# An output product begun before the last gate, modulation columns placed behind the emitted blocks, and a norm whose small operations read PSUM

## The chip, the cores and the metric

The kernel runs on one core of one Trainium2 chip. The metric is the device time of one execution in microseconds (us). Engines are named as the profile names them: PE (TensorE, matmuls; PEld loads its weights), DVE (VectorE), ACT (ScalarE), POOL (GpSimd) and SP, which here only issues DMAs. SBUF is the on-chip memory, PSUM the banks into which PE writes and from which DVE and ACT read; POOL does not touch PSUM here.

## What is computed

A two-layer backbone on 512 tokens of width 1024. Layer 0 mixes tokens with a state-space branch (SSD) and eight heads of gated linear attention (GLA); layer 1 with a convolution module. A convolutional gated MLP follows each. Both sub-blocks end in a residual and a layer norm, and per-channel modulation columns are made from the conditioning vector:

```python
for l in range(DEPTH):                                   # DEPTH = 2
    m = (s_c @ ada_w[l] + ada_b[l]).reshape(-1, 6, 1, D_MODEL)
    h = modulate(x, m[:, 0], m[:, 1])
    if l % 2 == 0:
        y, yc = even_mixer(h, hc, mix_w_in[e], ..., mix_w_out[e], ctx_next)
    else:
        y = conformer_conv(h, *conf)
    x = layer_norm(ALPHA * x + m[:, 2] * y, post_ln_g[l, 0], post_ln_b[l, 0])
    x = layer_norm(ALPHA * x + m[:, 5] * conv_glu_ffn(modulate(x, m[:, 3], m[:, 4]), *ffn, rows, GRID_W),
                   post_ln_g[l, 1], post_ln_b[l, 1])

def merge(s, y, o):                                      # end of even_mixer
    ys = rms_norm(y * silu(z), ssd_nw, SSD_GROUPS)
    os_ = rms_norm(o, hg_nw, HG_HEADS) * silu(g)
    return concatenate([ys, os_], axis=-1) @ w_out
```

## The kernel before

Activations lie channel-major: a 1024-wide tensor is eight tiles of 128 channels by 512 tokens. Every fp32 product is made of three matmuls on operands split into a high and a low part: high weight times high activation, high times low, low times high (L214 to L216, `mm3w`, weights stationary; L233 to L235, `mm3a`, activations stationary). The weights come as one stream of 128x512 tiles in a fixed order: SP loads `wraw`, ACT casts the high part `whi` (L184), and the low part `wlo` (L188) is a subtraction on DVE, or on POOL once `lo_pool` is set.

A modulation column is made by `ada` (L266 to L274): a 512 KB DMA into one of two `ada` buffers and one DVE instruction (L273) of 128x1024 with an accumulator. `ada_some(n)` issues the next n columns of a list, to follow the instruction that `self.after` names. Before, each GLA head takes one at each of its seven levels, `merge` takes 16, and the FFN of layer 0 the rest.

A GLA head ends with levels (`lev` matmuls; L746 copies them under a mask into `p`; L748 to L754 update `kq` and `t`), then, for two directions, transposes of `kq` (`pk`, L764), a copy to `kt` (ACT L766), state updates (`pu`, L769) and outputs (`po`). `merge` then emits 16 blocks of the output product's activations (transposes `pt`, L818; `ohi` on ACT, L821; `olo` on DVE, L822), the last four after a gate whose second factor `sg` comes from the last projection (`psz`) and whose multiplications are L791. The output product runs 16 blocks deep over five columns into five PSUM banks (`psg`), then the residuals (L903) free them, and `project` makes the three other columns: one whole (`ps`), two by halves of 256 tokens (`psh`).

The norm is made by halves as well. `ln_add` accumulates the sum and the sum of squares (`a`, L924 and L925). `ln_sums` has PE sum over channels (`sm`, L938), then a chain of small DVE operations on 128x2 (mean, variance, and a reciprocal root by three Newton steps, `rsqrt`, L255 to L261). `ln_spread` has PE spread mean and root over the channels (`pb`, L954), and `normalise` applies them (L1019 and L1020; in the last norm L959 and L960), with the split for the next product (L1022 to L1027). `stats_later(n1, n2)` inserts sums and spreading behind so many of the `mm3w` calls of the product that runs meanwhile; `post` does it for the second half inside the next product.

The program is written in one order; a scheduler then sets the order of each engine's instructions by its own model, within what the buffers, the data and `issue_after` allow. Each engine runs its instructions in that order.

Of the kernel before, what the change touches and what calls it, by code (L numbers as in the profile page):

```python
# [17 lines left out]
P = 128  # L18
# [129 lines left out]
class Net:  # L148
# [104 lines left out]
    def rsqrt(self, y, v, tmp, itmp):  # L253
# [4 lines left out]
        for _ in range(3):  # L258
            ve.tensor_tensor(out=tmp, in0=y, in1=y, op=ALU.mult)
            ve.scalar_tensor_tensor(out=tmp, in0=tmp, scalar=-0.5, in1=v, op0=ALU.mult, op1=ALU.mult)  # L260
            ve.scalar_tensor_tensor(out=y, in0=tmp, scalar=1.5, in1=y, op0=ALU.add, op1=ALU.mult)  # L261
# [422 lines left out]
    def gla(self, h, v, act, actc, qs, o, so, gp, gd, mm, lv, mi):  # L684
# [53 lines left out]
        while m < P:  # L738
# [16 lines left out]
            if lev < self.ADA_HEAD:  # L755
                self.ada_some(1)
# [27 lines left out]
    ADA_HEAD, ADA_OUT, ADA_DOWN = 7, 16, 5  # L784
# [8 lines left out]
    def merge(self, mx, ox, y, o, so, acth):  # L793
# [9 lines left out]
        mm = ps_.enter_context(self.pool("mm", 5, PSUM))  # L803
# [10 lines left out]
        def emit(src, wname, half, off):  # L814
            for i in range(4):
# [6 lines left out]
                nc.vector.scalar_tensor_tensor(out=olo[:, n, :], in0=pt[:].rearrange("p c t -> p (c t)"), scalar=col,  # L822
# [7 lines left out]
        for c, ps in enumerate(proj(C_G, 1)):  # L830
            nc.scalar.activation(out=sg[:, c, :], in_=ps, func=AF.Silu)
        self.gate(o, sg, r, 4, 4)
# [6 lines left out]
        es = self.es  # L839
        self.x = es.enter_context(self.pool("x", side="right")).tile([P, KT, T], F32, name="x")  # L840
        self.work = es.enter_context(self.pool("work", 4, side="right"))
        self.mm = es.enter_context(self.pool("mm", 5, PSUM))
        self.lnps = es.enter_context(self.pool("lnps", 1, PSUM))
        for k in range(KT):
            nc.sync.dma_start(out=self.x[:, k, :], in_=self.A["xT"][k])
            nc.scalar.mul(self.x[:, k, :], self.x[:, k, :], ALPHA)
        self.lo_pool = True
        ln = self.ln_start()
        bk = [self.mm.tile([P, T], F32, tag="mm", name="psg") for _ in range(NW1)]
        self.ada_some(self.ADA_OUT)  # L850
        for k in range(16):
            for i in range(NW1):
                self.mm3w(bk[i], self.wblock(("wout", k * P, i * P)), (ohi[:, k, :], olo[:, k, :]), k == 0, k == 15)
# [9 lines left out]
    def project(self, ln, w, act, kt, layer, j, tail, then=None, first=0):  # L863
# [10 lines left out]
        for t0, t1 in HALVES:  # L874
# [8 lines left out]
            if t1 < T:  # L883
                self.stats_later(ln, t0, t1, 6, 8)
# [45 lines left out]
    def ln_sums(self, ln, t0, t1):  # L930
# [4 lines left out]
        sm = self.lnps.tile([P, 2 * n], F32, tag="sm", name="sm")  # L935
# [5 lines left out]
        nc.vector.tensor_scalar_mul(st, sm, 1.0 / D)  # L941
        mu = st[:, 0:n]
        nc.vector.tensor_tensor(out=tmp, in0=mu, in1=mu, op=ALU.mult)
        nc.vector.scalar_tensor_tensor(out=v, in0=st[:, n:], scalar=EPS, in1=tmp, op0=ALU.add, op1=ALU.subtract)
# [305 lines left out]
```

## Time and profile before

| quantity | value |
|---|---|
| runs of the kernel, median (lowest to highest) | 1761.66 us (1760.66 to 1762.17) |
| profiled execution, its own time | 1762.31 us |
| its span | 1760.5 us |
| mean granted PE clock | 0.99 |
| instructions in the trace | 26474 |
| modulation column DMAs | 104 of 512 KB, 3.6 us to landing |
| weight tile DMAs | 488 of 256 KB, 2.7 us to landing |

Busy shares are averages over stages. What bounds a stage is read from the waits of the engine that is busiest there, and from windows that show the granted clock beside the busy times. In a timeline row stand the start, the duration, engine, line, operation and tiles, and in brackets the idle time before it with the instruction that ended it.

### The profile page before, as it was taken

To read this page: it belongs to the slowest core of one execution; us is meant where nothing else is said; L and a number is where in the kernel's file an instruction comes from. 1 tells how busy PE (TensorE), PEld (TensorE's weight loads), DVE (VectorE), ACT (ScalarE), POOL (GpSimd) and SP (SyncE) were. 2 spreads that over 40 slices of the span, in tenths; PEclk is the share of its full clock that TensorE was granted. 3 is DMA by queue.
4 is the path that set the end of the run, shared out by engine and by line. 5 is a ranking of instruction groups with operands and counts; after the bars stand their busy time and mean duration, and the time that the engine had idled before them with its cause. 6 is when DMAs were issued, how large, how long until landed. Compare 5 with 4: busy or idle time off the path is not lost. (4 is left out here: it accounts for less than half of the span.)

```text
span 1760.5 us, 26474 instructions
## 1 busy us (share of the span) xinstructions
PE 1707.3 (97%) x9574; PEld 1465.3 (83%) x9574; DVE 1247.9 (71%) x2368; ACT 850.5 (48%) x1713; POOL 525.8 (30%) x436
## 2 busy tenths in 40 slices
PE   6999999999999999999999999999999999999996
PEld 5987768989899987887888888988898888888886
DVE  7778988969695996378777731488788777776125
ACT  4556775354444544364333422499534743333233
POOL 4400000000000003544444444533415444444451
PEclk9999999999999999999999999999999999999998
DMA  9621102434343448423333333322203233333331
GB/s 365 239 66 48 31 19 89 135 119 154 109 144 120 133 139 277 134 85 114 108 108 108 109 112 96 102 73 60 61 26 90 85 96 98 100 96 96 96 107 61
DMA packets 92194, 194.02 MB, mean 110 GB/s; under 512 B 10496, under 2 KB 13568, under 8 KB 92064
## 3 DMA queue, kind: packets, MB, share of 16 engines
q1 hardware_dynamic: 92016, 192.21, 35.0%
q8 instruction: 75, 1.23, 0.3%
q14 instruction: 55, 0.45, 0.1%
q0 software_dynamic: 48, 0.13, 0.0%
HBM read 190.21 MB, written 2.10 MB: 109 GB/s over the span
## 5 line engine op out<-in xcount | busy, mean ns | idle before, releaser
L188 POOL TENSOR_TENSOR wlo<-wraw,whi 128x512 fp32r<-128x512 f32 x388 | 510.0, 1318 | 1188.5 <-ACT whi L184 1171.6
L184 ACT CAST whi<-wraw 128x512 fp32r<-128x512 f32 x488 | 300.9, 619 | 509.2 <-PE ps L215 254.0
L214 PE MATMUL ps<-h1hi,whi 128*128 128x512 f32 x768 | 299.9, 391 | 2.0 <-DVE acc L1066 1.9
L216 PE MATMUL ps<-h1hi,wlo 128*128 128x512 f32 x768 | 299.6, 390 | 0.6 <-POOL wlo L188 0.6
L215 PE MATMUL ps<-h1lo,whi 128*128 128x512 f32 x768 | 299.6, 390 | 0.0
L1066 DVE SCALAR_TENSOR_TENSOR acc<-ps,pcol,acc 128x441 f32<-128x441 f32 (+2 forms) x320 | 222.4, 695 | 57.5 <-ACT acc L1058 47.9
L214 PEld LDWEIGHTS ps<-h1hi,whi 128*128 128x128 f32 x768 | 144.5, 188 | 32.2 <-ACT acc L1058 2.3
L216 PEld LDWEIGHTS ps<-h1hi,wlo 128*128 128x128 f32 x768 | 144.6, 188 | 31.2 <-POOL wlo L188 1.1
L215 PEld LDWEIGHTS ps<-h1lo,whi 128*128 128x128 f32 x768 | 144.7, 188 | 29.5
L273 DVE CUSTOM_DVE_ANT_0 junk<-ada,sc,pcol 128x1024 bf16<-128x1024 f32 x80 | 105.8, 1322 | 14.8 <-DMA ada<-adaw 14.6
L903 DVE SCALAR_TENSOR_TENSOR x<-ps,mod,x 128x512 f32<-128x512 f32 x14 | 10.5, 750 | 146.7 <-PE ps L216 146.7
L215 PE MATMUL ps<-glo,whi 128*128 128x512 f32 x264 | 102.7, 389 | 0.0
L214 PE MATMUL ps<-ghi,whi 128*128 128x512 f32 x264 | 102.7, 389 | 0.0
L216 PE MATMUL ps<-ghi,wlo 128*128 128x512 f32 x264 | 102.7, 389 | 0.0
L1158 DVE SCALAR_TENSOR_TENSOR cr<-u,pcol,cr 128x511 f32<-128x511 f32 (+20 forms) x156 | 97.7, 699 | 1.7 <-ACT cr L1141 1.5
L214 PE MATMUL ps<-hhi,whi 128*128 128x512 f32 x240 | 98.0, 408 | 0.0
L215 PE MATMUL ps<-hlo,whi 128*128 128x512 f32 x240 | 96.5, 402 | 0.0
L216 PE MATMUL ps<-hhi,wlo 128*128 128x512 f32 x240 | 96.0, 400 | 0.0
L188 DVE TENSOR_TENSOR wlo<-wraw,whi 128x512 fp32r<-128x512 f32 x100 | 68.0, 686 | 26.0 <-ACT whi L184 25.2
L979 DVE TENSOR_TENSOR glo<-acc,ghi 128x512 fp32r<-128x512 f32 x44 | 56.4, 1282 | 29.7 <-ACT ghi L978 29.6
L233 PE MATMUL psz<-whi,hhi 128*128 128x256 f32 (+1 forms) x224 | 67.5, 302 | 0.0
L234 PE MATMUL psz<-wlo,hhi 128*128 128x256 f32 (+1 forms) x224 | 67.1, 300 | 0.0
(353 smaller groups left out, 4168.0 us busy)
## 6 DMA issues: line engine op xcount, KB each, us to landing
wraw<-wst SPq DMA_DIRECT2D x488, 256.0 KB, 2.7
ada<-adaw SPq DMA_DIRECT2D x104, 512.0 KB, 3.6
xk<-xT SPq DMA_DIRECT2D x8, 256.0 KB, 7.8
x<-xT SPq DMA_DIRECT2D x8, 256.0 KB, 5.1
out<-n SPq DMA_DIRECT2D x16, 128.0 KB, 1.7
xk<-ctxT SPq DMA_DIRECT2D x8, 128.0 KB, 4.0
sc<-rows SPq DMA_DIRECT2D x1, 512.0 KB, 3.5
scc<-rows SPq DMA_DIRECT2D x1, 512.0 KB, 7.6
```

Source lines behind the costliest of these rows:

```text
L184: nc.scalar.copy(hi, raw)
L188: eng.tensor_tensor(out=lo, in0=raw, in1=hi.bitcast(F32), op=ALU.subtract)
L214: mm(ps, w[0], a[0], start=start, stop=False)
L215: mm(ps, w[0], a[1], start=False, stop=False)
L216: mm(ps, w[1], a[0], start=False, stop=stop)
L233: mm(ps, a[0], w[0], start=start, stop=False)
L234: mm(ps, a[0], w[1], start=False, stop=False)
L273: nc.vector.tensor_tensor_reduce(out=junk, in0=raw, in1=self.sc if cond is None else cond, scale=1.0, scalar=self.pc("adab", n), op0=ALU.m ...
L903: self.after = self.nc.vector.scalar_tensor_tensor(out=r, in0=ps, scalar=self.modc(layer, j, i), in1=r, op0=ALU.mult, op1=ALU.add)
L979: return nc.vector.tensor_tensor(out=lo, in0=x, in1=hi.bitcast(F32), op=ALU.subtract)
L1066: nc.vector.scalar_tensor_tensor(out=o, in0=grid(pg)[:, r0 + dy - 1:r1 + dy - 1, c0 + dx - 1:c1 + dx - 1], scalar=wcol(dy, dx), in1=o, op0 ...
L1158: nc.vector.scalar_tensor_tensor(out=acc[:, t0:t1], in0=u[:, t0 + d:t1 + d], scalar=self.pc("cdw", tap * 8 + i), in1=acc[:, t0:t1], op0=AL ...
```

## The change

Six edits.

1. Each of the first six GLA heads takes eight columns (two at the first level), the last two heads four each.
2. In `merge`, all banks come from one pool of five (`mm`) that lives on; the output product's first six of 16 blocks are written ahead of the last gate. The pool `mi` stays.
3. The columns of `merge` are twelve and follow the last `olo`; the ten other blocks, the loads of x and the start of the norm follow them in the program. `lo_pool` is set after the emits as before.
4. The sums and the spreading of the first half stand behind 9 and 12 more calls of `mm3w`, formerly 6 and 8. In `post`, the second half's statistics and normalisation are written directly, without the hook into the next product.
5. The small operations of `ln_sums` read the sums in PSUM, the root's iterate y lies in PSUM too, and each instruction has at most one operand in SBUF that is a tensor beside one in PSUM; the addition of EPS is an instruction of its own. Fifteen operations stand where fourteen stood.
6. The FFN of layer 0 takes a column at every third tile instead of every fourth.

```diff
@@ rsqrt
-        for _ in range(3):
-            ve.tensor_tensor(out=tmp, in0=y, in1=y, op=ALU.mult)
-            ve.scalar_tensor_tensor(out=tmp, in0=tmp, scalar=-0.5, in1=v, op0=ALU.mult, op1=ALU.mult)
-            ve.scalar_tensor_tensor(out=y, in0=tmp, scalar=1.5, in1=y, op0=ALU.add, op1=ALU.mult)
+        for i in range(3):
+            ve.tensor_tensor(out=tmp, in0=v, in1=y, op=ALU.mult)
+            ve.scalar_tensor_tensor(out=tmp, in0=tmp, scalar=-0.5, in1=y, op0=ALU.mult, op1=ALU.mult)
+            ve.scalar_tensor_tensor(out=out if out is not None and i == 2 else y, in0=tmp, scalar=1.5, in1=y, op0=ALU.add, op1=ALU.mult)
@@ gla
-            if lev < self.ADA_HEAD:
-                self.ada_some(1)
+            if h < 6 or lev < 4:
+                self.ada_some(2 if h < 6 and lev == 0 else 1)
@@ merge
-    ADA_HEAD, ADA_OUT, ADA_DOWN = 7, 16, 5
+    ADA_OUT, ADA_DOWN = 12, 5
...
-        mm = ps_.enter_context(self.pool("mm", 5, PSUM))
+        es = self.es
+        mm = self.mm = es.enter_context(self.pool("mm", 5, PSUM))
...
-                nc.vector.scalar_tensor_tensor(out=olo[:, n, :], ...
+                self.after = nc.vector.scalar_tensor_tensor(out=olo[:, n, :], ...
...
+        bk = [mm.tile([P, T], F32, tag="mm", name="psg") for _ in range(NW1)]
+        def out(k0, k1):
+            for k in range(k0, k1):
+                for i in range(NW1):
+                    self.mm3w(bk[i], self.wblock(("wout", k * P, i * P)), (ohi[:, k, :], olo[:, k, :]), k == 0, k == 15)
+        out(0, 6)
         self.gate(o, sg, r, 4, 4)
         emit(o, "hnw", 1, 8)
...
+        self.lo_pool = True
+        self.ada_some(self.ADA_OUT)
+        out(6, 16)
         for k in range(KT):
             nc.sync.dma_start(out=self.x[:, k, :], in_=self.A["xT"][k])
             nc.scalar.mul(self.x[:, k, :], self.x[:, k, :], ALPHA)
-        self.lo_pool = True
         ln = self.ln_start()
-        bk = [self.mm.tile([P, T], F32, tag="mm", name="psg") for _ in range(NW1)]
-        self.ada_some(self.ADA_OUT)
-        for k in range(16):
-            for i in range(NW1):
-                self.mm3w(bk[i], self.wblock(("wout", k * P, i * P)), (ohi[:, k, :], olo[:, k, :]), k == 0, k == 15)
@@ project
-                self.stats_later(ln, t0, t1, 6, 8)
+                self.stats_later(ln, t0, t1, 9, 12)
@@ ln_sums
-        sm = self.lnps.tile([P, 2 * n], F32, tag="sm", name="sm")
+        sm = self.lnps.tile([P, 3 * n], F32, tag="sm", name="sm")
...
-        nc.vector.tensor_scalar_mul(st, sm, 1.0 / D)
-        mu = st[:, 0:n]
-        nc.vector.tensor_tensor(out=tmp, in0=mu, in1=mu, op=ALU.mult)
-        nc.vector.scalar_tensor_tensor(out=v, in0=st[:, n:], scalar=EPS, in1=tmp, op0=ALU.add, op1=ALU.subtract)
-        self.rsqrt(r, v, tmp, it)
+        nc.vector.tensor_scalar_mul(st, sm[:, 0:2 * n], 1.0 / D)
+        nc.vector.scalar_tensor_tensor(out=tmp, in0=sm[:, 0:n], scalar=1.0 / D, in1=st[:, 0:n], op0=ALU.mult, op1=ALU.mult)
+        nc.vector.scalar_tensor_tensor(out=v, in0=sm[:, n:2 * n], scalar=1.0 / D, in1=tmp, op0=ALU.mult, op1=ALU.subtract)
+        nc.vector.tensor_scalar_add(v, v, EPS)
+        self.rsqrt(sm[:, 2 * n:], v, tmp, it, r)
@@ post
-        self.stats_later(ln, *HALVES[1], 7, 9, lambda p: normalise(*HALVES[1], p))
-        if last:
-            self.flush()
+        normalise(*HALVES[1], self.ln_stats(ln, *HALVES[1]))
@@ ffn
-            if layer == DEPTH - 1 or i % 4 == 0:
+            if layer == DEPTH - 1 or i % 3 == 0:
```

How the scheduled order moves is shown at three places. The first is PE at the end of the last GLA head. Before, the two pairs of transposes and state updates stand together:

```order
L233 MATMUL psz<-whi_6561,hhi 128x256
L744 MATMUL lev<-kq,kg 128x128 x4
L764 MATMUL pk<-tri,kq 128x128 x3
L769 MATMUL pu<-v,kt 128x128 x3
L764 MATMUL pk<-tri,kq 128x128 x3
L769 MATMUL pu<-v,kt 128x128 x3
L234 MATMUL psz<-wlo_6563,hhi 128x256
```

In the changed kernel (line numbers from here on are its own, one to seven higher) five projection matmuls stand inside each pair:

```order
L744 MATMUL lev<-kq,kg 128x128 x4
L765 MATMUL pk<-tri,kq 128x128 x3
L234 MATMUL psz<-wlo_6575,hhi 128x256
L235 MATMUL psz<-whi_6573,hlo 128x256
L233 MATMUL psz<-whi_6573,hhi 128x256
L234 MATMUL psz<-wlo_6575,hhi 128x256
L235 MATMUL psz<-whi_6573,hlo 128x256
L770 MATMUL pu<-v,kt 128x128 x3
L765 MATMUL pk<-tri,kq 128x128 x3
```

The projection matmuls have moved behind the transposes; on DVE the update of `kq` that the transposes need stands ahead of the last masked copy.

The second is DVE around the last gate. Before, columns stand between the two factors of the gate and between the emitted blocks:

```order
L791 TENSOR_TENSOR o<-o,r 128x4x128
L273 ISA junk,mod<-ada_7181,sc,pcol 128x1024
L273 ISA mod 128x1
...
L188 TENSOR_TENSOR wlo_7075<-wraw_7071,whi_7073 128x512
L273 ISA junk,mod<-ada_7189,sc,pcol 128x1024
L273 ISA mod 128x1
L273 ISA junk,mod<-ada_7193,sc,pcol 128x1024
L273 ISA mod 128x1
L791 TENSOR_TENSOR o<-o,sg 128x4x128 x4
L822 SCALAR_TENSOR_TENSOR olo<-pt,pcol,ohi 128x512 x3
```

In the changed kernel the gate (now L792) has weight splits around it, and the twelve columns follow the emitted blocks (now L824) up to the residuals (now L909):

```order
L188 TENSOR_TENSOR wlo_7075<-wraw_7071,whi_7073 128x512
L792 TENSOR_TENSOR o<-o,sg 128x4x128
L188 TENSOR_TENSOR wlo_7102<-wraw_7098,whi_7100 128x512
L792 TENSOR_TENSOR o<-o,sg 128x4x128 x3
...
L188 TENSOR_TENSOR wlo_7228<-wraw_7224,whi_7226 128x512
L824 SCALAR_TENSOR_TENSOR olo<-pt,pcol,ohi 128x512 x4
L273 ISA junk,mod<-ada_7285,sc,pcol 128x1024
...
L273 ISA junk,mod<-ada_7329,sc,pcol 128x1024
L273 ISA mod 128x1
L909 SCALAR_TENSOR_TENSOR x<-psg,mod,x 128x512 x3
```

The columns have moved from ahead of the gate to ahead of the residuals, and eight weight splits have moved from POOL to DVE. On PE, 90 matmuls of `psg` stand ahead of the first `pt` of the last gate, where six stood, and 150 behind or among the four emits. On SP, pairs of column loads stand between the weight loads of the blocks seven to 16.

The third is DVE in the last norm, the chain of the first half. Before:

```order
L941 TENSOR_SCALAR st<-sm 128x4
L943 TENSOR_TENSOR vt<-st 128x2
L944 SCALAR_TENSOR_TENSOR v<-st,vt 128x2
L256 TENSOR_SCALAR vi<-v 128x2
L257 TENSOR_SCALAR rs<-vi 128x2
L259 TENSOR_TENSOR vt<-rs 128x2
L260 SCALAR_TENSOR_TENSOR vt<-vt,v 128x2
L261 SCALAR_TENSOR_TENSOR rs<-vt,rs 128x2
```

In the changed kernel:

```order
L948 TENSOR_SCALAR st<-sm 128x4
L949 SCALAR_TENSOR_TENSOR vt<-sm,st 128x2
L950 SCALAR_TENSOR_TENSOR v<-sm,vt 128x2
L951 TENSOR_SCALAR v<-v 128x2
L256 TENSOR_SCALAR vi<-v 128x2
L257 TENSOR_SCALAR sm<-vi 128x2
L259 TENSOR_TENSOR vt<-v,sm 128x2
L260 SCALAR_TENSOR_TENSOR vt<-vt,sm 128x2
L261 SCALAR_TENSOR_TENSOR sm<-vt,sm 128x2
```

The iterate `rs` has become a part of `sm`, and every operation with two tensor inputs has one of them there. On PE, the sums of this norm's first half stand nine matmuls of 128x256 later, and 36 of them (formerly 24) stand between the sums and the spreading. In the first norm of layer 0, the spreading of the second half's root stands behind all 72 half-width matmuls that use the first half; before, it stood among them.

More of the change, by code (lines that the diff above doesn't have):

```diff
@@ L251, in pc, with rsqrt @@
         return self.pcol[:, c:c + 1]
-    def rsqrt(self, y, v, tmp, itmp):
+    def rsqrt(self, y, v, tmp, itmp, out=None):
         ve = self.nc.vector
@@ L821, in emit @@
                 nc.scalar.activation(out=ohi[:, n, :], in_=pt[:].rearrange("p c t -> p (c t)"), func=AF.Identity, scale=col)
-                nc.vector.scalar_tensor_tensor(out=olo[:, n, :], in0=pt[:].rearrange("p c t -> p (c t)"), scalar=col,
+                self.after = nc.vector.scalar_tensor_tensor(out=olo[:, n, :], in0=pt[:].rearrange("p c t -> p (c t)"), scalar=col,
                                                in1=ohi[:, n, :].bitcast(F32), op0=ALU.mult, op1=ALU.subtract)
@@ L837, in merge @@
         ox.close()
-        es = self.es
         self.x = es.enter_context(self.pool("x", side="right")).tile([P, KT, T], F32, name="x")
         self.work = es.enter_context(self.pool("work", 4, side="right"))
-        self.mm = es.enter_context(self.pool("mm", 5, PSUM))
         self.lnps = es.enter_context(self.pool("lnps", 1, PSUM))
+        self.lo_pool = True
+        self.ada_some(self.ADA_OUT)
+        out(6, 16)
         for k in range(KT):
```

## The prediction

> **What bounds the kernel now.** I read the page's busy table first, then TensorE's (PE's) waits, then windows around the largest of them.
>
> ```profile
> PE 1707.3 (97%) x9574; PEld 1465.3 (83%) x9574; DVE 1247.9 (71%) x2368; ACT 850.5 (48%) x1713; POOL 525.8 (30%) x436
> ```
>
> PE works 97% of the span and no matmul is removed, so the change can win only what PE idles or runs at a lower clock. The waits of PE say where it idles (wait: microseconds in total, times, longest):
>
> ```profile
> PE pb L954 <- DVE rs L261: 11.4, 6, 2.6
> PE pt L818 <- DVE o L791: 3.0, 1, 3.0
> PE sm L938 <- DVE a L924: 2.6, 2, 1.5
> PE ps L214 <- DVE acc L1066: 1.9, 1, 1.9
> PE pk L764 <- DVE kq L748: 1.4, 1, 1.4
> PE pu L769 <- ACT kt L766: 1.1, 2, 0.6
> ```
>
> The first row is the half-norms: PE waits for VectorE's (DVE's) reciprocal root before it can spread it. The second is the last gate, and the last two are the end of the last GLA head. The windows (PE, PEld, DVE, ACT, POOL busy, then granted clock, DMA share, GB/s) show that an idle stretch costs more than itself:
>
> ```profile
> 620.00:640.00 20.00, 17.43 (x144) 16.56 (x143) 18.17 (x46) 7.19 (x19) 0.00 (x0) 1.00 0.36 119
> 660.00:680.00 20.00, 16.98 (x78) 14.12 (x77) 16.17 (x29) 8.05 (x14) 1.26 (x1) 0.91 0.77 260
> 755.00:775.00 20.00, 17.95 (x150) 17.63 (x150) 17.23 (x48) 12.68 (x26) 10.50 (x8) 1.00 0.37 106
> 795.00:815.00 20.00, 18.09 (x73) 14.44 (x72) 18.83 (x32) 9.05 (x14) 8.51 (x7) 0.91 0.41 119
> 1120.00:1140.00 20.00, 17.44 (x134) 17.20 (x133) 12.92 (x32) 7.78 (x15) 8.96 (x7) 0.91 0.27 74
> 1358.00:1378.00 20.00, 15.04 (x99) 14.46 (x98) 18.13 (x54) 11.38 (x22) 9.06 (x7) 0.83 0.34 97
> 1726.00:1746.00 20.00, 16.55 (x124) 16.10 (x124) 14.25 (x35) 8.07 (x15) 6.92 (x6) 0.91 0.15 53
> ```
>
> A granted clock of 0.91 over 20 us is 20 x 0.09 = 1.8 us of lost matmul time. It stands beside idle stretches of 2 to 3 us and not beside the 1.65 us one near 760. So I price such a stretch at its length plus 1.8. [...]
>
> **GLA tail.** In the order of after, PE's last two pk, pu pairs have projection matmuls between them, and the last L748 stands ahead of the last copy of levels (L746), with no modulation column behind.
>
> ```profile
> 627.09 0.55 PE L764 MATMUL pk<-tri,kq 128*128 128x128 f32 x3 [1.39 <-DVE kq L748]
> 628.21 0.94 PE L769 MATMUL pu<-v,kt 128*128 128x128 f32 x6 [0.57 <-ACT kt L766]
> 630.04 0.94 PE L769 MATMUL pu<-v,kt 128*128 128x128 f32 x6 [0.57 <-ACT kt L766]
> ```
>
> 1.39 + 0.57 + 0.57 = 2.5 us go; the window's idle time is 20 - 17.43 = 2.6. **-2.5**, bounds -2.6 and 0. Heads 0 to 5 take one more column each, 1.32 us of DVE (row of L273 below); PE shows no wait there, so I count 0. If DVE's slack is gone, six columns cost up to 6 x 1.32 = +7.9; no wait row of these heads speaks for it.
>
> **Merge: the last gate.** What holds it is a column that waits for its DMA and stands ahead of the gate's last multiplications:
>
> ```profile
> 670.82 0.39 PE L214 MATMUL psg<-ohi,whi 128*128 128x512 f32 x1
> 671.05 0.39 PE L215 MATMUL psg<-olo,whi 128*128 128x512 f32 x1
> ...
> 673.01 1.60 DVE L273 CUSTOM_DVE_ANT_0 junk<-ada,sc,pcol 128x1024 bf16<-128x1024 f32 x1 [2.00 <-DMA ada<-adaw]
> ...
> 674.53 2.49 DVE L791 TENSOR_TENSOR o<-o,sg 128x512 f32<-128x512 f32 x4
> ...
> 675.36 1.09 PE L818 MATMUL pt<-tri,o 128*128 128x128 f32 x4 [3.02 <-DVE o L791]
> ```
>
> After, no column stands there, and 90 output matmuls stand ahead of the first transposition: 90 x 0.227 (two rows above: 671.05 - 670.82 = 0.23) = 20.4 us of cover for a gate of 2.5 us and eight weight splits that moved from POOL to DVE (8 x 0.69 = 5.5, by the first of the groups below). The 3.02 us and its 1.8 us of clock go: -4.8. The next thing late is the emitted blocks; PE does 4 transpositions where ACT and DVE must follow, which I charge 0.1. **-4.7**, bounds -4.8 and -3.0 (clock lost elsewhere in the stage).
>
> **Merge: the twelve columns.** They now follow the last emitted block on DVE, and only behind them come the residuals (L903) that free the five banks of the output product. PE's next product needs the first of those banks.
>
> ```profile
> L188 DVE TENSOR_TENSOR wlo<-wraw,whi 128x512 fp32r<-128x512 f32 x100 | 68.0, 686 | 26.0 <-ACT whi L184 25.2
> L273 DVE CUSTOM_DVE_ANT_0 junk<-ada,sc,pcol 128x1024 bf16<-128x1024 f32 x80 | 105.8, 1322 | 14.8 <-DMA ada<-adaw 14.6
> L903 DVE SCALAR_TENSOR_TENSOR x<-ps,mod,x 128x512 f32<-128x512 f32 x14 | 10.5, 750 | 146.7 <-PE ps L216 146.7
> ```
>
> ```profile
> DMA to landing us min/median/max: 3.4/4.3/7.1
> ```
>
> The last row is the landing time of the columns' DMAs between 660 and 735. There are two buffers, filled side by side, so the columns go in rounds of two, and a round is the cycle of one buffer: landing 4.3, reading 1.32, and an estimated 0.2 for the accumulator's read and the next issue, 5.8 us. Counted from the first of the 90 matmuls, emitting ends at about 20.4 + 2.5 + 1 = 24; the first pair is loaded (2.6), five rounds follow (29.2): 55.8, and five small operations between them 1.0: 56.8. PE reaches the next product at 20.4 + 2.5 (transpositions) + 150 x 0.227 = 57.0, and the first residual must end there (0.75 + 0.1), so the columns must end by 56.1. At 4.3 us PE stalls 0.7; each further microsecond of landing adds 5. I take 4.55: **+2.0**, bounds 0 (landing 4.1) and +14.7 (landing 7.1). DMAs queued on SP behind a column that waits for its buffer (weights, x) arrive later too; the same rounds pace them. Columns of GLA heads and of the first FFN only change place: their DVE time stays 80 x 1.32.
>
> **Half-norm chains.** In the last norm the small operations with two SBUF inputs stand still while POOL runs a weight split; the one that reads PSUM doesn't:
>
> ```profile
> 1726.68 0.16 DVE L941 TENSOR_SCALAR st<-sm 128x4 f32<-128x4 f32 x1 [1.55 <-PE sm L938]
> 1726.88 0.94 DVE L943 TENSOR_TENSOR vt<-st 128x2 f32<-128x2 f32 x1
> ...
> 1728.84 1.28 POOL L188 TENSOR_TENSOR wlo<-wraw,whi 128x512 fp32r<-128x512 f32 x1 [1.04 <-ACT whi L184]
> 1728.85 1.29 DVE L261 SCALAR_TENSOR_TENSOR rs<-vt,rs 128x2 f32<-128x2 f32 x1
> ...
> 1730.28 1.26 POOL L188 TENSOR_TENSOR wlo<-wraw,whi 128x512 fp32r<-128x512 f32 x1 [0.16 <-ACT whi L184]
> 1730.37 1.19 DVE L260 SCALAR_TENSOR_TENSOR vt<-vt,v 128x2 f32<-128x2 f32 x1
> ...
> 1732.40 0.43 PE L954 MATMUL pb<-tri,rs 128*128 128x128 f32 x2 [2.56 <-DVE rs L261]
> ```
>
> From 1726.68 to 1732.40 the chain takes 5.7 us. Without POOL, at the kernel's end, it takes 2.8:
>
> ```profile
> 1747.30 0.16 DVE L941 TENSOR_SCALAR st<-sm 128x4 f32<-128x4 f32 x1 [0.76 <-PE sm L938]
> ...
> 1750.07 0.69 PE L954 MATMUL pb<-tri,rs 128*128 128x128 f32 x2 [2.13 <-DVE rs L261]
> ```
>
> ```profile
> L1024 DVE TENSOR_SCALAR h<-x,cg,cb 128x256 f32<-128x256 f32 x12 | 6.5, 544 | 0.1
> ...
> L1027 DVE TENSOR_TENSOR h1lo<-h,h1hi 128x256 fp32r<-128x256 f32 x48 | 20.2, 420 | 9.5 <-ACT h L1026 9.1
> ```
>
> The two groups above are one arithmetic kind with its output in PSUM (h) and in SBUF. The new chain has one operation more (0.2) and three that write PSUM, each dearer by at most 0.544 - 0.420 = 0.12: 2.8 + 0.6 = 3.4 us. The cover ahead of the spreading grows, by the order, from 24 to 36 matmuls of 128x256, which start 0.12 apart:
>
> ```profile
> 1744.71 0.28 PE L215 MATMUL psh<-glo,whi 128*128 128x256 f32 x1
> 1744.83 0.28 PE L216 MATMUL psh<-ghi,wlo 128*128 128x256 f32 x1
> ```
>
> The cover goes from 2.9 to 4.3 us, so the 2.56 us stall closes. If every two-input operation is still held, the chain is 6.3 and the stall 2.0: then -0.6 only. [...]
>
> Five norms, each by itself. **First norm of layer 0: 0**, bounds -1.6 and +1.3: PE would gain 1.65 at 760, but later waits for DVE anyway (row of acc L1066, 1.9 us; DVE 18.83 of 20 busy at 795), while the second half's spreading now stands behind all first-half matmuls, without cover. **Second norm of layer 0: -3.7**: stall 2.56 plus clock 1.8 is 4.4, and 0.7 is kept for DVE; bounds -4.4 and -0.6. **Conformer norms: 0**, whose own code is untouched. **First norm of layer 1: 0**, bounds -3 and +1.5: DVE is busy 18.13 of 20 there. **Last norm: -2.4**: the same 4.4, of which I keep back 0.9, because the sums stand nine matmuls (9 x 0.12 = 1.1) later in PE's order, so that much less work is left behind them to cover DVE's sixteen first-half normalisations; -3.5. The second chain has no cover and is 0.6 longer, and ACT's last square, behind eight outputs in its order, is charged one output row's start distance of about 0.5. Bounds -3.8 and +0.5.
>
> **The sum**: -2.5 - 4.7 + 2.0 - 3.7 - 2.4 = -11.3, from the profiled execution's 1762.31 (span 1760.5 and 1.8 around it) to 1751.0. The median of the runs, 1761.66, is 0.65 lower: **1750.4**.
>
> **Rivals.** *Columns late*: landing averages 5.5 us instead of 4.55, so PE stalls 4.7 more and loses 1.8 of clock: 1756.9. For it: landings from 3.4 to 7.1. Against: median 4.3. *The norms give nothing*: operations stay held, or DVE, 71% busy in all and over 90% at two norms, gives the gain back: +6.1 gives 1756.5. *All closes*: columns in time (-2), and layer 0's and layer 1's first norm gain 1.6 and 3: 1743.8. *Slower*: one mechanism, the twelve columns in front of the residuals. The stall with its clock eats the other gains of 13.3 when it reaches 11.5, that is a mean landing of 0.7 + 5 x (landing - 4.3) = 11.5, 6.5 us; at the longest landing seen, 7.1, it is 14.7 + 1.8 = 16.5 and the time 1761.66 - 13.3 + 16.5 = 1764.9; with the norms giving nothing as well, 1771. *The change does not do what it says* (the scheduler spreads the columns again): the order shows it done, so this has no share.
>
> **How the numbers follow.** Forecast 0.48, columns late 0.16, norms nothing 0.14, all closes 0.08, the column stall at its upper end 0.14. About 0.2% (3.5 us) is what a measurement of this kernel tells from no change: faster is below 1758.1, slower above 1765.2. Late columns and idle norms together reach 1763, so of their 0.30 I put 0.09 within; of the last case 0.06 lies within and 0.08 above. That gives faster 0.77, same 0.15, slower 0.08. The range reaches from all-closes to past the two middle rivals, 1743.5 to 1761.
>
> **What would show it.** Right: PE's wait for o in front of pt gone; granted clock 1.00 in the merge and 0.95 or more at the second and last norm; the spreading's total wait under 6 us. Wrong: a wait of the product behind the residual (ps for L903) over 3 us, with DVE waiting for the columns' DMA; two-input or SBUF-only operations of the chain still at 1.2 us beside POOL; a new wait of the second half's spreading.

## The result and the profile after

The changed kernel takes 1750.39 us (median of four runs, 1750.07 to 1751.54) where the kernel before, timed beside it, took 1761.16 (1759.2 to 1762.17): a ratio of 0.9941, 95% interval 0.9924 to 0.9959. The forecast was 1750.4. Its profiled execution took 1750.37, with a span of 1748.6 against 1760.5 before. The total came out as forecast; the terms of the sum did not, and the experiments below say which. One of the 18 runs of the kernel before in the first series of experiments was a slow one of 3314.95 us; the ratios leave it out.

The first row is the page's busy table of the changed kernel, the others are PE's waits (total, times, longest).

```profile
PE 1700.7 (97%) x9574; PEld 1459.9 (83%) x9574; DVE 1244.6 (71%) x2386; ACT 850.4 (49%) x1713; POOL 518.2 (30%) x428
```

```profile
PE pb L961 <- DVE rs L261: 5.0, 4, 2.3
PE sm L945 <- DVE a L930: 3.7, 3, 1.9
PE psg L214 <- ACT h1hi L1029: 3.4, 3, 1.6
PE ps L214 <- ACT whi L184: 3.4, 1, 3.4
PE pc L214 <- DVE cr L1168: 2.0, 1, 2.0
...
PE pu L770 <- ACT kt L767: 0.6, 1, 0.6
```

The wait for the gate (pt for o, 3.0) and that of the last head's transposes (pk for kq, 1.4) are gone; the wait for the root fell from 11.4 to 5.0. New is one wait of 3.4 before the product `ps`, and `psg` waits longer for `h1hi` (3.4 for 1.8). The sums wait as long as before (4.0 for 3.9, both lines of `a` together).

Of the 5.0 that the root still costs, 2.3 are the closing chain, and 2.0 are the first half of the first norm of layer 1, which waited 2.3 before:

```profile
1349.89 0.16 DVE L948 TENSOR_SCALAR st<-sm 128x4 f32<-128x4 f32 x1 [0.66 <-PE sm L945]
...
1352.70 0.48 DVE L909 SCALAR_TENSOR_TENSOR x<-psh,mod,x 128x256 f32<-128x256 f32 x1
...
1353.21 1.45 DVE L930 TENSOR_TENSOR a<-a,x 128x256 f32<-128x256 f32 x1
...
1354.65 1.46 DVE L931 TENSOR_TENSOR a<-a,sq 128x256 f32<-128x256 f32 x1
...
1356.62 0.43 PE L961 MATMUL pb<-tri,rs 128*128 128x128 f32 x2 [2.01 <-DVE rs L261]
```

Here DVE works a residual and its two sums (L909, L930, L931) between the small operations, and from the first of them to the spreading it takes 6.7 us, where the prediction has 3.4.

The windows (PE, PEld, DVE, ACT, POOL busy, clock, DMA share, GB/s) show the same:

```profile
620.00:640.00 20.00, 20.00 (x168) 19.55 (x168) 17.21 (x45) 7.98 (x20) 0.00 (x0) 1.00 0.21 67
660.00:680.00 20.00, 20.00 (x90) 16.57 (x89) 7.86 (x12) 6.91 (x12) 0.00 (x0) 1.00 0.46 155
720.00:740.00 20.00, 16.63 (x67) 13.27 (x66) 13.97 (x19) 9.54 (x16) 10.98 (x7) 0.91 0.61 195
...
1115.00:1135.00 20.00, 20.00 (x170) 20.00 (x170) 11.49 (x34) 9.23 (x18) 10.88 (x9) 1.00 0.32 93
1345.00:1365.00 20.00, 16.25 (x121) 15.67 (x120) 16.63 (x43) 9.40 (x19) 10.28 (x8) 0.91 0.39 114
1714.00:1734.00 20.00, 18.82 (x159) 18.65 (x158) 13.14 (x40) 9.45 (x17) 7.68 (x6) 1.00 0.13 47
```

The gate, the second norm of layer 0 and the last norm, at 0.91 before, now run at a full clock; the end of the heads did so already, and has lost its idle time. At 720 the new wait stands, with a clock of 0.91.

Stage by stage, the start of the same instruction in both traces gives what each stage gained. The stages end at the first transposition of `merge`, the residual of the sixth output column, the ninth high part `ghi` of the first FFN, the first residual of the conformer's second product, the fifth `ghi` of the second FFN (the 27th of both), and the end of the span. The start differs from that of the kernel before by -0.7 to +1.9 us in the thirteen other profiles, so its +1.0 tells nothing of the change.

| stage | forecast | changed minus before, us |
|---|---|---|
| start, up to the first `lev` matmul | 0 | +1.0 |
| GLA heads | -2.5 | -4.2 |
| merge | -4.7 + 2.0 | +0.9 |
| first norm of layer 0 | 0 | -2.4 |
| second norm of layer 0, conformer's first part | -3.7 | -2.3 |
| first norm of layer 1 | 0 | -1.4 |
| last norm and end | -2.4 | -3.6 |
| sum | -11.3 | -12.0 |

### The profile page after: what moved, and what is told of

It reads as the page before. It is cut to its first block, busy times and chain, and to the rows that moved or that the text cites. A ratio compares the mean times of both kernels' runs of the same rounds, so it can differ in the third digit from the quotient of the medians.

```text
span 1748.6 us, 26467 instructions
## 1 busy us (share of the span) xinstructions
PE 1700.7 (97%) x9574; PEld 1459.9 (83%) x9574; DVE 1244.6 (71%) x2386; ACT 850.4 (49%) x1713; POOL 518.2 (30%) x428
## 4 chain that ended last, share of the span: by engine, by line
PE 88%; DVE 6%; ACT 2%; DMA 1%; issue 1%; POOL 0%; SPq 0%; DVEq 0%; POOLq 0%; ACTq 0%
PE ps L214 18%; PE ps L216 18%; PE ps L215 18%; PE lev L744 3%; PE psz L234 2%; PE psz L233 2%; PE psz L235 2%; PE psh L214 2%; PE psh L216 2%; PE psh L215 2%; PE seg L645 2%; PE psv L234 1%; PE psv L235 1%; PE psv L233 1%; PE psg L215 1%; PE pc L215 1%
## 5 line engine op out<-in xcount | busy, mean ns | idle before, releaser
L188 POOL TENSOR_TENSOR wlo<-wraw,whi 128x512 fp32r<-128x512 f32 x380 | 502.4, 1327 | 1183.6 <-ACT whi L184 1164.0
L273 DVE CUSTOM_DVE_ANT_0 junk<-ada,sc,pcol 128x1024 bf16<-128x1024 f32 x80 | 108.3, 1354 | 15.8 <-DMA ada<-adaw 15.5
L909 DVE SCALAR_TENSOR_TENSOR x<-ps,mod,x 128x512 f32<-128x512 f32 x14 | 10.5, 751 | 141.6 <-PE ps L216 141.6
L188 DVE TENSOR_TENSOR wlo<-wraw,whi 128x512 fp32r<-128x512 f32 x108 | 73.8, 689 | 42.7 <-ACT whi L184 42.3
```

The lines of the kernel that those rows point to most:

```text
L188: eng.tensor_tensor(out=lo, in0=raw, in1=hi.bitcast(F32), op=ALU.subtract)
L273: nc.vector.tensor_tensor_reduce(out=junk, in0=raw, in1=self.sc if cond is None else cond, scale=1.0, scalar=self.pc("adab", n), op0=ALU.m ...
```

## The experiments

Below, "idle" is the sum of PE's gaps over 0.15 us in a stage of one profile, and the number behind the + counts the stretches of 3.41 us with a granted clock of 0.5 (half clocks) that fall into it. By estimate (half of 3.41) one such stretch costs up to 1.7 us, where PE has work throughout; in the one at 1292.21 in the changed kernel the matmuls of 128x256 start 0.21 us apart, ahead of it 0.12. Not counted is the last stretch of every profile, 12.6 to 14.7 us from the closing chain to the end, where PE has almost no work. "Norm 0.1" is the stage of the first norm of layer 0, "norm 0.2" that of its second norm with the conformer's first part, and so on.

| kernel | GLA | merge | norm 0.1 | norm 0.2 | norm 1.1 | last | median, us |
|---|---|---|---|---|---|---|---|
| before | 2.5+0 | 3.0+1 | 4.9+1 | 7.1+2 | 5.6+2 | 6.1+1 | 1761.16 |
| changed | 0.6+0 | 3.4+1 | 3.5+0 | 5.7+1 | 5.3+1 | 3.7+0 | 1750.39 |
| only small operations | 2.5+0 | 3.0+1 | 4.9+1 | 5.0+1 | 3.9+1 | 3.7+0 | 1753.26 |
| only cover | 2.5+2 | 3.0+0 | 4.4+2 | 6.1+0 | 5.8+2 | 4.9+0 | 1758.67 |
| only heads | 0.6+0 | 3.1+0 | 4.9+0 | 7.0+1 | 5.9+2 | 6.1+1 | 1755.57 |
| only merge | 2.5+0 | 3.0+0 | 4.9+0 | 7.0+1 | 5.9+2 | 6.1+1 | 1761.65 |
| changed, old small operations | 0.6+0 | 2.4+1 | 4.0+1 | 6.3+0 | 4.8+2 | 4.8+0 | 1751.78 |
| changed, no columns in merge | 0.6+0 | 0.0+0 | 3.5+0 | 5.7+2 | 6.0+2 | 3.7+0 | 1747.28 |
| changed, x first | 0.6+0 | 6.5+2 | 3.3+1 | 5.6+1 | 6.0+1 | 3.7+0 | 1754.16 |
| changed, second half hooked | 0.6+0 | 2.5+0 | 4.7+1 | 5.5+2 | 6.8+2 | 3.7+0 | 1754.93 |
| no columns, old order | 0.6+0 | 1.4+0 | 3.3+1 | 5.7+2 | 5.3+1 | 3.7+0 | 1747.60 |
| no columns, 6 and 8 | 0.6+0 | 0.0+0 | 4.0+3 | 4.3+1 | 3.0+0 | 3.7+0 | 1745.89 |
| changed, again | 0.6+0 | 3.4+2 | 3.4+0 | 5.5+1 | 5.3+1 | 3.7+0 | 1750.45 |
| changed, four buffers | 0.6+0 | 0.0+0 | 3.5+0 | 5.7+2 | 5.9+1 | 3.7+0 | 1747.42 |

The medians of the experiments come from three series; the kernel before had 1763.12 in the first (the four "only" kernels), 1762.81 in the second (the next four) and 1763.86 in the third (the last four). Where a size counts, the ratio to the kernel before in the same series stands in the text. The changed kernel has two ratios: 0.9941 in its own series, and 0.9931 (0.9914 to 0.9948) in the third. A difference of 0.001 between series, 1.8 us, can thus be chance alone.

By their ratios the four "only" kernels gain 9.7, 3.9, 7.6 and 0.7 us, 21.9 together; all edits at once gain 10.4 or 12.2. The first two close the same stall; what else they share is not shown. The second half's direct writing was not run alone.

### Which part closed the stall before the spreading

Only the small operations:

```diff
 # before.py
-        self.rsqrt(r, v, tmp, it)
+        self.rsqrt(sm[:, 2 * n:], v, tmp, it, r)   # with the new ln_sums and rsqrt
```

> The kernel before with only the new small operations of the norm (PSUM operands, fifteen instead of fourteen). Theory: DVE's two-input operations stand still beside POOL's weight splits only when both inputs lie in SBUF, so the chain shortens from 5.7 to about 2.9 us and 24 matmuls (2.9 us) just cover it: the stall before the spreading falls from 2.56 to under 0.5 us at the second norm of layer 0 and at the last norm, the clock is 1.0 there, and the median is 4 to 7 us under before. Rival: the longer cover of 36 matmuls closed the stall, so the chain is still over 4 us or a stall of 1 to 2.5 us stays, and the median is within 2 us of before.

Ratio 0.9945 (0.9928 to 0.9962). Its waits:

```profile
PE pb L955 <- DVE rs L261: 2.7, 2, 2.3
```

Of 11.4 us, 2.7 are left, and 2.3 of these are the closing chain, which has nothing to cover it; the first norm of layer 1 waits 0.45, where the changed kernel with its longer cover waits 2.0. The old cover of 24 matmuls is enough. The gain of 9.7 us by the ratio is more than the 4 to 7 expected. Between the two profiles, idle time fell by 6.2 us (from 29.2 to 23.0, the sums of the rows above), and three half clocks fewer are at most 5.1.

Only the cover:

```diff
 # before.py
-                self.stats_later(ln, t0, t1, 6, 8)
+                self.stats_later(ln, t0, t1, 9, 12)
```

> The kernel before with only the later places of the first half's sums and spreading (9 and 12 instead of 6 and 8 calls). Theory that the chain's length is what counts: a chain of 5.7 us against a cover of 4.3 leaves a stall of 1.2 to 1.6 us at the second norm of layer 0 and at the last norm; the median is 1 to 4 us under before. Rival (cover decides): the stall is under 0.5 us and the median 4 to 7 us under before.

Ratio 0.9978 (0.9966 to 0.9989), 3.9 us and within what was expected. The second norm of layer 0 in its timeline (DVE, POOL and the spreading):

```profile
1130.18 4.15 POOL L188 TENSOR_TENSOR wlo<-wraw,whi 128x512 fp32r<-128x512 f32 x3 [1.06 <-ACT whi L184]
1130.30 1.20 DVE L260 SCALAR_TENSOR_TENSOR vt<-vt,v 128x2 f32<-128x2 f32 x1
...
1131.73 1.21 DVE L259 TENSOR_TENSOR vt<-rs 128x2 f32<-128x2 f32 x1
...
1134.99 0.43 PE L954 MATMUL pb<-tri,rs 128*128 128x128 f32 x2 [1.29 <-DVE rs L261]
```

The chain is as long as before and 1.29 us stay, as the theory had it (1.2 to 1.6). The changed kernel's last norm, beside POOL as well:

```profile
1719.37 0.16 DVE L948 TENSOR_SCALAR st<-sm 128x4 f32<-128x4 f32 x1 [2.63 <-PE sm L945]
1719.56 0.16 DVE L949 SCALAR_TENSOR_TENSOR vt<-sm,st 128x2 f32<-128x2 f32 x1
...
1720.56 0.16 DVE L259 TENSOR_TENSOR vt<-v,sm 128x2 f32<-128x2 f32 x1
1720.75 0.16 DVE L260 SCALAR_TENSOR_TENSOR vt<-vt,sm 128x2 f32<-128x2 f32 x1
...
1722.11 0.16 DVE L261 SCALAR_TENSOR_TENSOR rs<-vt,sm 128x2 f32<-128x2 f32 x1
```

```profile
1720.45 2.73 POOL L188 TENSOR_TENSOR wlo<-wraw,whi 128x512 fp32r<-128x512 f32 x2 [1.06 <-ACT whi L184]
```

The same L259 and L260 now take 0.16 us inside a POOL subtraction, and the chain 2.9 (1719.37 to 1722.27). With one input in PSUM they are not held there; with both in SBUF they took 1.21 and 1.20 in the rows above. The new addition of EPS is a `tensor_scalar` from SBUF to SBUF, and it is still held: in the kernel with only the small operations it took 0.17 us at the median of its ten places, and 0.56 at the two that fell into a POOL subtraction. One of them ends with the subtraction, at 1128.0:

```profile
1125.46 2.54 POOL L188 TENSOR_TENSOR wlo<-wraw,whi 128x512 fp32r<-128x512 f32 x2 [8.25 <-ACT whi L184]
1127.46 0.56 DVE L945 TENSOR_SCALAR v<-v 128x2 f32<-128x2 f32 x1
```

The three writes to PSUM cost about 0.01 us each at most (at the median of the changed kernel L261 takes 166 ns into `sm` and 157 into `rs`).

The changed kernel with the old small operations:

```diff
 # after.py
-        self.rsqrt(sm[:, 2 * n:], v, tmp, it, r)
+        self.rsqrt(r, v, tmp, it)                  # with the old ln_sums and rsqrt
```

> The changed kernel with the old small operations of the norm (fourteen, all in SBUF). Theory: beside POOL's splits the chain is 5 to 6 us again, the 36 matmuls cover 4.3 of it, and PE stalls 1 to 2 us before the spreading at the second norm of layer 0 and at the last norm; 2 to 6 us slower than the changed kernel in all. Rival (the cover did it): under 1 us slower.

```profile
PE pb L960 <- DVE rs L261: 7.2, 6, 2.1
```

The stall of 1.29 us returned at both norms, as expected, but the ratio to before is 0.9942 (0.9927 to 0.9956), beside 0.9941 and 0.9931 of the changed kernel: no difference clear of noise, where 2 to 6 us were expected. The wait in the merge was 2.4 instead of 3.4 and layer 1's first norm idled 4.8 instead of 5.3, so 1.5 of the 2.6 came back there; why is not shown. In the changed kernel, then, the cover alone nearly does; on the kernel before, the small operations are the stronger.

### The GLA heads

```diff
 # before.py
-            if lev < self.ADA_HEAD:
-                self.ada_some(1)
+            if h < 6 or lev < 4:
+                self.ada_some(2 if h < 6 and lev == 0 else 1)
```

> The kernel before with only the new numbers of modulation columns per GLA head (eight in six heads, four in two). Theory: the three waits at the last head's end (1.39, 0.57, 0.57 us) go, because no column stands there and projection matmuls stand between; PE's lost time in the GLA stage falls by 2.5 to 4.2 us, the median by 2 to 5 us. Rival: the waits go only with the new merge, or the extra columns in six heads cost as much as is saved: within 1.5 us of before.

The three waits went and the stage took 4.2 us less, exactly as in the changed kernel, so this part needs no other. Ratio 0.9957 (0.9941 to 0.9973): 7.6 us, more than the stage gives; the profile has three half clocks fewer than that of before, at waits that this kernel shares with it. Eight columns instead of seven in six heads cost at most one new wait of 0.57 us for `kt`, in an early head. Of the 4.2, gaps over 0.15 us explain 2.0 (2.5 before, 0.6 now). The other 2.2 are no gaps: for the same matmuls PE counts as busy 342.63 us before and 340.40 here, at a clock of 1.00 in both. Why their spacing shrank is not shown.

### The merge

Only the merge's part:

```diff
 # before.py, with the new merge()
-    ADA_HEAD, ADA_OUT, ADA_DOWN = 7, 16, 5
+    ADA_HEAD, ADA_OUT, ADA_DOWN = 7, 12, 5
-            if layer == DEPTH - 1 or i % 4 == 0:
+            if layer == DEPTH - 1 or i % 3 == 0:
```

> The kernel before with only the merge part (output product's first six blocks ahead of the gate, one pool, twelve columns behind the emitted blocks, a column at every third FFN tile). Theory: the 3.0 us wait at the gate and its clock loss go (4.7), and a wait of 3 to 3.5 us before the next product with a clock loss of 1.7 takes their place, so the median is within 2 us of before. Rival: the columns behind the emitted blocks cost under 1 us when the rest is unchanged, and the median is 3 to 5 us under before.

Ratio 0.9996 (0.9984 to 1.0008). The gate's wait went and this one came:

```profile
PE ps L214 <- DVE x L908: 3.0, 1, 3.0
```

That is the residual behind the columns, as the prediction's term for the columns has it. In the changed kernel the profile names the weight cast on ACT instead. Its timeline:

```profile
722.46 2.07 DVE L273 CUSTOM_DVE_ANT_0 junk<-ada,sc,pcol 128x1024 bf16<-128x1024 f32 x1 [1.46 <-DMA ada<-adaw]
...
725.15 1.58 DVE L273 CUSTOM_DVE_ANT_0 junk<-ada,sc,pcol 128x1024 bf16<-128x1024 f32 x1 [0.62 <-DMA ada<-adaw]
...
726.66 2.06 DVE L909 SCALAR_TENSOR_TENSOR x<-psg,mod,x 128x512 f32<-128x512 f32 x3
```

```profile
726.90 0.60 ACT L184 CAST whi<-wraw 128x512 fp32r<-128x512 f32 x1
```

```profile
727.55 0.47 PE L214 MATMUL ps<-ohi,whi 128*128 128x512 f32 x1 [3.37 <-ACT whi L184]
```

The first of three residuals ends at about 727.4 (726.66 and 0.74), the cast at 727.50, PE goes on at 727.55. Two things were late by the same amount, and the profile names only the later. To part them, x's loads and their scaling, which stand ahead of the cast on ACT, were put before the columns:

```diff
 # after.py
+        for k in range(KT):
+            nc.sync.dma_start(out=self.x[:, k, :], in_=self.A["xT"][k])
+            nc.scalar.mul(self.x[:, k, :], self.x[:, k, :], ALPHA)
         self.ada_some(self.ADA_OUT)
         out(6, 16)
-        for k in range(KT):
-            nc.sync.dma_start(out=self.x[:, k, :], in_=self.A["xT"][k])
-            nc.scalar.mul(self.x[:, k, :], self.x[:, k, :], ALPHA)
```

> The changed kernel with the eight loads of x and their scaling on ACT written ahead of the twelve columns. Theory A: the residuals behind the columns on DVE (the first ends at 727.4, PE goes on at 727.55) hold PE by themselves, so the wait stays 2.5 us or more and the time within 1.5 us of the changed kernel. Theory B: the weight cast on ACT behind x's late loads holds PE (the wait ends with the cast), so the wait falls below 1.5 us, and the time by 2 to 5 us.

```profile
PE ps L214 <- DVE x L909: 6.5, 1, 6.5
```

This is theory A in its cause: the profile names the residual and no longer the cast. Both theories missed the size. The eight loads now stand together ahead of the weights and the columns on SP, the last column is read at 728.70 instead of 725.15, and the ratio is 0.9953 (0.9938 to 0.9968). Then the columns were taken out of the merge:

```diff
 # after.py
-    ADA_OUT, ADA_DOWN = 12, 5
+    ADA_OUT, ADA_DOWN = 0, 5
```

> The changed kernel with no columns in the merge: its twelve go to the down product of layer 0's FFN, sixteen there in all. Theory: the twelve columns hold both the residuals on DVE and the loads behind them on SP, so the wait of 3.4 us before the next product and the half clock behind it go: 4 to 5.5 us under the changed kernel, about 1745.5. Rival: the columns only move the wait, and the down product (five columns and one residual for each 15 us) shows a new wait of the same size: within 1.5 us of the changed kernel.

No wait is left in the merge, and the down product, which took the twelve, shows none. Ratio 0.9915 (0.9900 to 0.9929) beside 0.9941 and 0.9931, whose intervals overlap with it. By medians 3.1 us are gained, less than the 4 to 5.5 expected; its profile has half clocks in other places. Four buffers instead of two do the same with the columns in place:

```diff
 # after.py, merge()
-        self.adap = op.enter_context(self.pool("adap", 2))
+        self.adap = op.enter_context(self.pool("adap", 4))
```

> The changed kernel with four buffers for the columns in the merge instead of two. Theory: the rounds of two buffers (landing about 4.3 and reading 1.3) set the pace, so with four the twelve columns end at least 8 us earlier, the wait before the next product falls under 0.5 us, and 2 to 5 us go. Rival: DMA bandwidth or the loads queued on SP set it, and over 2 us of wait stay.

Ratio 0.9911 (0.9894 to 0.9928), no wait. In the same series the changed kernel has 0.9931, and its runs (1748.67 to 1752.83) all lie above these (1745.91 to 1747.79). The group of the columns in the merge, in the changed kernel and with four buffers (minimum, median and maximum in ns, first and last start; the second row is the landing of their DMAs):

```profile
L273 DVE CUSTOM_DVE_ANT_0 junk<-ada,sc,pcol x12: 1270/1432/2310, 692.2 to 725.2; 128x1024 bf16<-128x1024 f32 x12
...
DMA to landing us min/median/max: 3.5/4.2/4.9
```

```profile
L273 DVE CUSTOM_DVE_ANT_0 junk<-ada,sc,pcol x12: 1272/1286/2354, 690.8 to 712.4; 128x1024 bf16<-128x1024 f32 x12
```

The rounds of two buffers set the pace: 33.0 us from the first to the last start, 21.6 with four, though single reads take up to 2.31 and 2.35. In the changed kernel the six reads that begin inside a POOL subtraction take 1.58 to 2.31 us, the six that begin outside one 1.27 to 1.29; each has two inputs in SBUF. Last, whether the output product must begin ahead of the gate once no column stands there:

```diff
 # after.py, with the merge() of before
-    ADA_OUT, ADA_DOWN = 12, 5
+    ADA_OUT, ADA_DOWN = 0, 5
```

> The changed kernel with the merge of before (all sixteen blocks behind the gate) and no columns in it. Theory: the column in front of the gate was most of the 3.0 us wait; without it the gate starts when its factor sg is there, and with only four output matmuls ahead PE waits 0.5 to 1.5 us for it, no half clock behind; no wait before the next product; 0 to 2 us over the kernel with no columns in the merge and with the new order. Rival: the gate itself needs the 90 matmuls of cover, so a wait of 2.5 us or more stays and 3 to 5 us are lost against it.

```profile
PE pt L819 <- DVE o L792: 1.4, 2, 0.8
```

The gate costs 1.4 us of idle time without cover, as expected, and the time is that of the new order (ratios 0.9916, interval 0.9898 to 0.9934, and 0.9915). With a column in front of the gate the wait was 3.0; the twelve columns made the new one.

### The second half's statistics, and the cover with the short chain

```diff
 # after.py
-        normalise(*HALVES[1], self.ln_stats(ln, *HALVES[1]))
+        self.stats_later(ln, *HALVES[1], 7, 9, lambda p: normalise(*HALVES[1], p))
+        if last:
+            self.flush()
```

> The changed kernel with the second half's statistics again hooked into the next product (after 7 and 9 calls). Theory: around the first norms DVE is the limit, so where the spreading stands changes the time by less than 1.5 us either way. Rival: the spreading without cover costs the waits for the second half (1.6 us at 776, 1.9 at 1137), and the hook takes 2 to 4 us off.

The rival is out: the ratio is 0.9955 (0.9939 to 0.9971), so the hook gains nothing. By medians it costs more than the theory's 1.5 us, but the intervals overlap with those of the changed kernel. The wait of the FFN's product for DVE (1.9 us at 801 in the kernel before, 0.4 in the changed one) is back:

```profile
PE ps L214 <- DVE acc L1073: 3.2, 2, 1.9
```

Writing the second half directly is worth about 2.7 us of idle time at the two first norms (4.7 and 6.8 against 3.5 and 5.3). The forecast took this part for a risk. Next, the short chain with the old cover, without columns in the merge:

```diff
 # after.py
-    ADA_OUT, ADA_DOWN = 12, 5
+    ADA_OUT, ADA_DOWN = 0, 5
-                self.stats_later(ln, t0, t1, 9, 12)
+                self.stats_later(ln, t0, t1, 6, 8)
```

> The changed kernel with no columns in the merge and with the sums and the spreading at the places of before (6 and 8). Theory: with the short chain of 2.9 us the cover of 24 matmuls is enough and sums that come earlier give DVE more time, so PE's idle time around the first norm of layer 1 falls from 6.0 to about 4 us and around the second norm of layer 0 from 5.7 to about 5; 1 to 4 us under the kernel with no columns. Rival: a chain with residuals inside it outgrows the shorter cover, the wait before the spreading returns (over 1 us at two norms), and it is 0 to 3 us over.

```profile
PE sm L945 <- DVE a L930: 4.4, 4, 1.7
PE pb L961 <- DVE rs L261: 2.7, 2, 2.3
```

The median is 1745.89 us, the ratio 0.9897 (0.9878 to 0.9916): this version beats both kernels, and all its runs lie below those of the changed kernel in this series. With the short chain, then, the later places cost idle time (15.5 us here in all stages, 19.5 with no columns and the later places), though the two ratios' intervals overlap: the root's wait at layer 1's first norm is 0.44 instead of 2.0, and that of the sums at layer 0's second norm 0.80 instead of 1.93. Layer 1's first norm idles 3.0 us and layer 0's second 4.3; layer 0's first pays for it, since its sums now wait 1.69 us for DVE. Late places for that norm and early ones for the others were not tried.

### The same kernel again

> The changed kernel itself in another execution. Theory: PE's clock halves for 3.4 us after a window of a fixed 3.41 us raster in which PE idled about 1.9 us or more, and the raster starts anew by chance in each execution: the waits keep their lengths to 0.1 us, but the number and places of the half clocks differ, and none follows a window that idled under 1.8. Rival: the half clocks belong to the waits, so the same ones (behind the product's wait at 724, in the second norm's and the first norm of layer 1) come again.

```profile
PE ps L214 <- DVE x L909: 3.4, 1, 3.4
```

The median is 1750.45, and every wait behind the start keeps its length to 0.1 us. This time the profile names the residual, not the cast, for the same 3.38 us, and settles which of the two holds PE, for the cast ends only after PE has gone on:

```profile
727.83 0.60 ACT L184 CAST whi<-wraw 128x512 fp32r<-128x512 f32 x1
728.15 0.77 PE L214 MATMUL ps<-ohi,whi 128*128 128x512 f32 x1 [3.38 <-DVE x L909]
```

The clock halved in the same stages, but twice behind this wait instead of once. So half of the rival holds; what decides is seen better at one wait that no kernel here changes, in the last section.

## Why the prediction was right in the sum, and where it wasn't

- **What bounds the kernel** held in the main: gains and losses are PE's waits and half clocks, but for 2.2 us in the heads.
- **The clock, 1.8 for each of three closed waits**, 5.4 of the forecast's 11.3: the step from one profile's half clocks to a price for each wait failed. The same wait of 3.0 us at the gate has a half clock in the profile of before and none in those with only the cover and only the heads, and in the profile of before `pc` idles 2.00 us without one. The two profiles have seven half clocks and three; how many of the four the change removed, two profiles cannot tell.
- **GLA tail, -2.5:** right in its mechanism (the waits of 1.39 and 0.57 twice are gone with this part alone), mis-sized: the stage gave 4.2. The gaps over 0.15 us shrank by 2.0, since one of 0.57 came in an early head; the rest is a closer spacing of the same matmuls, which the prediction has no term for.
- **The last gate, -4.7:** right, the wait and its clock loss went. But the cover of 90 matmuls was only a part of it: without a column in front, the old order waits 1.4 of the 3.0, and its time is the same.
- **The twelve columns, +2.0:** the mechanism was right (rounds of two buffers, the residual behind them, PE waiting for its bank), the size was not: the wait is 3.4 us, and 1.7 of clock loss (3.41 us at 0.50, by estimate) came with it. The landing time was near the assumed 4.55 (3.5, 4.2 and 4.9 as minimum, median and maximum). What failed is the term for reading, 1.32 a column: the mean of the twelve is 1.63, for four that begin inside POOL's weight splits take 2.07 to 2.31. The columns ended 59.1 us after the first of the 90 matmuls (667.60 to 726.74) instead of 58.1, and PE was ready at 56.6 instead of 57.0. The clock loss was priced only in the rival.
- **The chain of small operations, 3.4 us:** it is 2.9 at the second norm of layer 0 and at the last; the writes to PSUM cost about 0.01 us each at most (L261, 166 ns against 157), and the reads nothing: L949, which reads `sm`, takes 159 ns at the median, L943 of the kernel before, with its inputs in SBUF, 160. The stall closed at both norms. That the cover was needed too was implied and is wrong: the short chain closes it with the old cover. At the first norm of layer 1, where DVE puts a residual between the operations, it takes 6.7 and the stall of 2.0 stays.
- **Second norm of layer 0, -3.7:** -2.3. The stall went, but the sums of the second half now wait 1.93 us for DVE, where 0.93 stood, more than the 0.7 kept back, and a half clock fell behind the conformer's untouched wait.
- **First norms, 0 and 0:** -2.4 and -1.4. The step "DVE is the limit there" failed: the FFN's wait for DVE at 801 fell from 1.9 to 0.4, and with it a half clock. The experiment with the hook shows that writing the second half directly did it; the late spreading costs no more than the hooked one (a wait of 0.17 us for 0.34 at layer 0, and none at layer 1 in either). Of layer 1's 1.4, idle time is 0.3 and the rest one half clock fewer.
- **Last norm, -2.4:** -3.6. The 0.9 kept back for DVE was not needed, and the closing chain waits 0.17 longer (2.30 for 2.13), not 0.6.

The profile lost 3.6 us against the forecast in the merge and 1.0 at the start, and gained 5.3 more than forecast in heads and norms. These errors cancel by chance.

## What to carry to other kernels

Look first at what stands in front of a short serial step on its own engine: with one column waiting for its DMA in front of the gate PE idled 3.0 us there, without it 1.4, and twelve of them in front of a residual made 3.4 of a step that costs nothing. Where a chain of small operations runs beside another engine's long subtractions, keep one input of each out of SBUF (here 0.16 us instead of 1.20 beside POOL); that was worth 9.7 us alone, and the longer cover 3.9; once the chain was short, the cover's later places only cost idle time. Where buffers set the pace of a stream, try more of them before a new order: in the changed kernel four instead of two took the new wait away. In the kernel before, four were not run.

## What the runs showed of the hardware that was not expected

In the traces of the kernel before and of the changed one the half clocks stand on a raster of 3.413 us: each lasts 3.413 us (one of the kernel before twice that), and they start whole numbers of it apart, 38, 96, 5, 65 and 106 in the kernel before (from 674.75 us on), 165 and 19 in the changed one (from 729.01). The origin of the raster is not the same: counted from the start of the span, a step of it falls at 2.3 us in the first, at 2.0 in the second, and in the second execution of the changed kernel at about 0.5 (by its matmuls, which start 0.21 us apart from 1294.1 on, 0.12 before). One wait, `pc` for `cr` in the conformer, is 2.0 us long in all fourteen profiles (1.97 to 2.01). Three windows on the raster around it, first in the kernel before, then in the changed one, with the rows of the wait:

```profile
1292.56:1295.98 3.42, 3.42 (x31) 3.42 (x31) 3.42 (x9) 0.00 (x0) 0.00 (x0) 1.00 0.00 0
1295.98:1299.39 3.41, 1.95 (x17) 1.73 (x15) 3.41 (x10) 0.00 (x0) 0.00 (x0) 1.00 0.00 0
1299.39:1302.80 3.41, 2.87 (x24) 2.88 (x25) 2.51 (x7) 0.83 (x2) 0.00 (x0) 1.00 0.00 0
```

```profile
1299.93 0.39 PE L214 MATMUL pc<-uhi,dhi 128*128 128x256 f32 x1 [2.00 <-DVE cr L1163]
```

```profile
1285.38:1288.79 3.41, 3.41 (x30) 3.36 (x29) 3.41 (x10) 0.00 (x0) 0.00 (x0) 1.00 0.00 0
1288.79:1292.20 3.41, 1.40 (x12) 1.24 (x11) 3.22 (x9) 0.42 (x1) 0.00 (x0) 1.00 0.00 0
1292.20:1295.62 3.42, 3.42 (x18) 3.42 (x18) 0.93 (x3) 0.42 (x1) 0.00 (x0) 0.50 0.00 0
```

```profile
1290.96 0.39 PE L214 MATMUL pc<-uhi,dhi 128*128 128x256 f32 x1 [2.01 <-DVE cr L1168]
```

Before, the wait lies across two windows (1.46 us idle in the fuller one) and the clock stays at 1.00. In the changed kernel all 2.01 us lie in one, and the next window runs at 0.50. Of the fourteen profiles six have 1.89 us or more of this wait in one window, and a half clock follows in each; eight have 1.83 or less, and none follows. The window at 1288.79 was not idle: PE has 1.40 us of work in it. In the norms a window with less idle time can halve the clock too (0.93 us at 1145.79 in the kernel before, where sums of 128x1 run), so 1.9 is a number of this wait, not a bound for all. So by estimate (2.0, and 1.7 for a half clock with work throughout) the same wait costs 2.0 or 3.7 us by where it falls, and the half clocks counted in one profile are no measure of a kernel. The runs of one kernel that the ratios use lie 1.5 to 10 us apart; that the raster makes a part of this spread was not measured.
